# Two layers' filter products side by side, adaLN inside the first k and q units, and k's norm moved: a startup rearranged

## The chip, the core and the metric

The kernel runs on one core of one Trainium2 chip, as one program launched once. The metric is the device time of an execution in microseconds (us). Engines are named as in the profile: PE does the matmuls (PEld loads their weights), DVE and ACT the elementwise work, POOL and SP here almost only issue DMA transfers. All 16 DMA engines of the core serve the queues of SP and POOL.

## The reference

One step of a two-layer model on 256 latent and 128 context tokens of width 2048. Per layer: a shift, a scale and a gate come from a conditioning vector (adaLN), the normalised input is modulated by them and projected, and two branches share the result.

```python
shift, scale, gate = jnp.split(silu(c) @ w_ada + b_ada, 3)
h = rmsnorm(x, norm_g) * (1.0 + scale) + shift
q, k, v, g_att, hy_in, g_hy = jnp.split(h @ w_in, ...)
q = rmsnorm(q per head, q_g); k = rmsnorm(k per head, k_g)    # latent tokens: rotary as well
att = attend(q, k and cached k, v and cached v) * silu(g_att)
hy = hyena(hy_in, ...) * silu(g_hy)                           # long convolution through an FFT
x = x + gate * (concat(att, hy) @ w_out)
```

The long convolution needs a filter per layer. A small network over position features gives 64 hidden values per position; these are multiplied by a 64 x 2048 matrix (a forward and a backward filter of 1024 channels), weighted by a decay window, folded into one centred filter and Fourier transformed:

```python
hdn = sin(freq * (sin(freq * (z @ f_w1 + f_b1)) @ f_w2 + f_b2))     # L x 64
h = (hdn @ f_w3) * (exp(-t * deltas) + 0.05)                        # L x 2048
hf = rfft(fold(h[:, :1024], h[:, 1024:]))
```

The filters depend on weights only, so both layers' filters can be made at any time before they are used.

## The kernel before, in words

All matmul weights arrive in *units* of 1 MB, each as two halves of 512 KB that go into one of seven raw buffers (`RAWB`). SP issues the loads, in the order in which the program emits them; a load waits until its buffer has been released. There are adaLN units (function `ada_mm`; an "a" in `START`), units of k, q and v (kind "b", `b_mm`), and units of the other projections, which make up the main stream with v and the rest of q (kinds "a" and "o", `a_mm`). For the b units and the main stream the raw half is split into a rounded part `hi` (ACT, line 192) and a remainder `lo` (DVE, line 198), which releases the raw buffer; three matmuls (lines 765 to 767) then make up one exact product. An adaLN unit is multiplied as it is: four products, each on its own 32 columns of PE (line 249), and the raw halves are released by PE itself. Four adaLN units make a chunk of 512 outputs; the last copies the sums (line 255), and one step later `ada_fin` transposes them (line 262) and adds the bias. When shift and scale of a quarter of the features are there, `make_h` (lines 410, 414, 417) makes the modulated input for four of the 16 feature tiles.

Startup handles 40 units in the order that the string `START` writes out: 17 adaLN units, then k and q units with groups of 4, 4, 2, 2, 2 and 1 adaLN units between them, then the last k and the last q unit. k and q each have four units, and each accumulates into three banks of PSUM (128 tokens each). The last two units count no longer as startup.

Each unit is a *step* of a planner written in Python. In a step the program emits the loads for which buffers have come free (`load_main`), the unit's matmuls, and then background work from a list with a cost for each item, as long as a budget lasts: 2.0 for an adaLN unit (`BUD`), 0.8 for a b unit (`EB`), and an item is begun while any budget is left. A second list, `urgent`, holds work with the step at which it is due. `drain_bg` empties all lists at once.

The background list at startup is the making of the filters. For a layer `l`, a half of the channels `hf`, a position block `t` (two latent, one context) and the sum or difference `s` of forward and backward filter:

- `filt_h` (line 482): one product on 64 rows of PE, those of layer `l` (line 487), multiplied by the window on DVE (line 489) into one of six pieces of `pieces[hf]`; for two of the six, a row with the bias is added (line 491, loaded by POOL, line 466).
- `filt_H` (line 496): the transform of the latent part: two products (line 499), a copy on ACT (line 502), two combinations on DVE (503, 504) back into the pieces.
- `filt_Hc` (line 509): the same of the context part, one product (511) and one ACT copy (512).
- `spill` (line 516) writes finished pieces to memory, 256 KB each, from where line 694 fetches them later. Layer 0's pieces go through POOL's queue as soon as they are done. Layer 1's stay in their buffers and go through SP's queue, all twelve in a row, after `drain_bg` at the last k unit.

The list runs layer 0 half 0, layer 0 half 1, layer 1 half 0, layer 1 half 1; products of one group are emitted between the transforms of the group before it. `pieces[1]` lies in P3 and P4; P4 also receives k when it leaves PSUM.

When k's fourth unit is done, `b_evac` copies the three token blocks out of PSUM (line 779) and puts three calls of `qk_norm` into `urgent`, for this step, the next and the one after. `qk_norm` squares (536), sums (538), takes the root, scales (546), multiplies by the gain (547) and applies the rotary (556 to 561, the latent blocks only); one step later `tr4` transposes the block on PE (528). q does the same one step behind. The main stream after it (from 217.3 us on, 1296 us) is not edited by the change.

Of the kernel before, what the change touches and what calls it, by code (L numbers as in the profile page):

```python
# [13 lines left out]
ALU = mybir.AluOpType  # L14
# [23 lines left out]
AB = 1  # L38
AB0 = 1
FIN = 0  # L40
MB = 0
EB = 0.8
W0, W1, W2, W3, W4 = 6, 8, 4, 24, 0
R_Q = [0, 0, 0, 0, 2, 2, 4, 5]
# [26 lines left out]
def step_kernel(ctx, tc, xT, vec, cst, delta, zfeat, fw, ada, wb, wc, wo, ck, cv, qk1, yT, nk, nv):  # L71
# [171 lines left out]
    def ada_mm(u):  # L243
        l, ch, kc = u.kw["l"], u.kw["ch"], u.kw["kc"]
        if kc == 0:
            ada_bank[0] = adap.tile([128, 512], F32, name="adab", tag="bk")
        part = ada_bank[0]
        for t in range(4):
            mm(part[32 * t:32 * t + 32, :], scT[:, kc * 4 + t, :], u.raw[t // 2][:, (t % 2) * 512:(t % 2 + 1) * 512],  # L249
               start=(kc == 0), stop=(kc == 3))  # L250
        for h in range(2):
            release(u, h)
        if kc == 3:
            sb = tt()
            nc.scalar.copy(sb, part)
            (fins if FIN else urgent).append((state["step"] + 1, lambda: ada_fin(l, ch, sb)))
# [206 lines left out]
                              in_=fw[33 + 64 * l:33 + 64 * l + 64, 0:64])  # L463

    def load_hrow(l, hf):
        nc.gpsimd.dma_start(out=hrow[hf], in_=fw[289:290, (2 * l + hf) * 512:(2 * l + hf + 1) * 512])

    def filt_prep():
        for hf in range(2):
            load_hrow(0, hf)  # L470
# [7 lines left out]
    hsd = {}  # L478
    pieces = [[P1[:, 0:512], P1[:, 512:1024], P1[:, 2560:3072], P2[:, 3072:3584], P2[:, 3584:4096], P3[:, 2048:2560]],
              [P3[:, 2560:3072]] + [P4[:, 512 * i:512 * (i + 1)] for i in range(5)]]  # L480

    def filt_h(l, hf, t, s):

        b = bg_bank()
        w = w3s if s == 0 else w3d
        pr = slice(64 * l, 64 * l + 64)
        mm(b, hd2[pr, t * 128:(t + 1) * 128], w[pr, hf * 512:(hf + 1) * 512], start=True, stop=True)  # L487
        dst = pieces[hf][t * 2 + s]
        nc.vector.tensor_tensor(dst, b, win[:, t, hf * 512:(hf + 1) * 512], ALU.mult)
        if s == 0 and t != 1:  # L490
            nc.vector.tensor_tensor(dst[0:1, :], dst[0:1, :], hrow[hf], ALU.add)
            if t == 2 and l == 0:
                load_hrow(1, hf)
        hsd[hf, t, s] = dst

    def filt_H(l, hf, s):
        bs = [bg_bank() for _ in range(2)]
        for e in range(2):
            mm(bs[e], FL[:, s, e, :], hsd[hf, e, s], start=True, stop=True)  # L499
        t = tt()  # L500
        o, o2 = hsd[hf, 0, s], hsd[hf, 1, s]
        nc.scalar.mul(t, bs[0], 1.0 / LAT)
        nc.vector.scalar_tensor_tensor(out=o, in0=bs[1], scalar=1.0 / LAT, in1=t, op0=ALU.mult, op1=ALU.add)
        nc.vector.scalar_tensor_tensor(out=o2, in0=bs[1], scalar=-1.0 / LAT if s == 0 else 1.0 / LAT, in1=t,
                                       op0=ALU.mult, op1=ALU.add if s == 0 else ALU.subtract)
        if l == 0:
            spill(l, hf, s, (0, 1))

    def filt_Hc(l, hf, s):
        b = bg_bank()  # L510
        mm(b, FC[:, s, :], hsd[hf, 2, s], start=True, stop=True)
        nc.scalar.mul(hsd[hf, 2, s], b, 1.0 / CTX)
        if l == 0:
            spill(l, hf, s, (2,))

    def spill(l, hf, s, ts):
        for t in ts:
            (nc.gpsimd if l == 0 else nc.sync).dma_start(out=Hd[l][hf][:, 2 * t + s, :], in_=pieces[hf][t * 2 + s])


    qT = P1.rearrange("p (h t) -> p h t", h=8)
# [230 lines left out]
    def b_mm(u):  # L752
# [3 lines left out]
        for h in range(2):  # L756
            wh = u.hi[h].rearrange("p (k n) -> p k n", k=2)
            wl = u.lo[h].rearrange("p (k n) -> p k n", k=2)
            for m in range(3):
                for k in range(2):  # L760
                    kt = kc * 4 + h * 2 + k
                    ms = slice(m * 128, (m + 1) * 128)
                    first = kt == 0
                    last = kt == 15
                    mm(accs[g][m], hh[:, kt, ms], wh[:, k, :], start=first, stop=False)  # L765
                    mm(accs[g][m], hh[:, kt, ms], wl[:, k, :], start=False, stop=False)  # L766
                    mm(accs[g][m], hl[:, kt, ms], wh[:, k, :], start=False, stop=last)  # L767
                if u.mid and (h, m) != (1, 2):
                    run_bg(MB)

    def b_evac(u):
        l, g, kc = u.kw["l"], u.kw["g"], u.kw["kc"]
# [2 lines left out]
        for m in range(3):  # L775
            if g == 3:
                v_evac(l, m, accs[g][m])
            else:
                nc.scalar.copy((P4 if g == 2 else P3)[:, m * 512:(m + 1) * 512], accs[g][m])
# [140 lines left out]
    with tc.manual_schedule():  # L920
# [8 lines left out]
        at(11, rstd1)  # L929
        at(12, have_rstd)  # L930
        hs_t, H_t = [], []
        for l in range(NL):
            for hf in range(2):
                hs_t.append([(0.86, lambda l=l, hf=hf, t=t, s=s: filt_h(l, hf, t, s))
                             for s in (1, 0) for t in range(3)])
                H_t.append([(1.7, lambda l=l, hf=hf, s=s: filt_H(l, hf, s)) for s in (1, 0)] +
                           [(0.86, lambda l=l, hf=hf, s=s: filt_Hc(l, hf, s)) for s in (1, 0)])
        order = list(hs_t[0])
        for n in range(4):
            nh = hs_t[n + 1] if n < 3 else [None] * 6  # L940
            for k in range(4):
                order += [H_t[n][k]] + nh[(0, 1, 3, 5)[k]:(1, 3, 5, 6)[k]]
        for e in order:
            if e is not None:
                add(e[1], e[0], 2)
        last = None
        for i, u in enumerate(units + mains):
            load_main()
            startup = i < n_start
            u.mid = startup  # L950
            if startup or u.kind != "ada":
                state["step"] += 1
            if u.kind == "ada":
# [16 lines left out]
            if u.kind == "b" and u.kw["g"] == 2:  # L970
                kc = u.kw["kc"]
                if l == 1 and kc == 0:
# [1 line left out]
                    make_h(l, [0])  # L974
                    make_h(l, [1])
                    make_h(l, [2, 3])
                if kc == 3 and l == 0:
                    drain_bg()
                    for hf in range(2):
# [151 lines left out]
```

## Time and profile before

| what | value |
|---|---|
| time, median of 3 runs | 1515.55 us (1514.62 to 1516.08) |
| the profiled execution's own time | 1515.29 us |
| its span in the profile | 1513.5 us |
| PE busy | 1476.8 us, 98% of the span |
| DVE busy | 980.7 us, 65% |
| ACT busy | 578.0 us, 38% |
| granted clock of PE, mean | 0.989 |
| first k matmul, first matmul behind the last q unit | 87.9 us, 191.7 us |

A line of groups reads: line, engine, operation, what it writes <- what it reads, shapes, count | busy time, mean ns of one | idle time of the engine before them and who ended it. A matrix product of 32-bit numbers shows as two records (two passes). A line of the timeline reads: start, length, engine, line, operation, and in brackets the idle time before it and its cause. A line of the chain of waits gives start, length and what the path to the end was doing. A line of the waits gives who waited, for whom, total time, how often, the longest. A row of the windows gives the stretch, its length, busy time (and count) of PE, PEld, DVE, ACT and POOL, the granted clock, the DMA engines' busy share and the rate in GB/s.

### The profile page before, as it was taken

The numbers are of one execution on the slowest core, as the hardware profiler recorded it, in microseconds if no ns is written. First come the engines' busy times: TensorE is split into PE (matmuls) and PEld (weight loads), VectorE is DVE, ScalarE is ACT, GpSimd is POOL, SyncE is SP. The second block draws the span as 40 slices with busy tenths as digits, with TensorE's granted clock in tenths as the row PEclk, the third lists the DMA queues.
The fourth block names the chain that finished last, engine by engine and source line by source line (L and its number), as shares of the span: only waits on it lengthen the run. The fifth ranks groups of instructions, "written<-read, shape, count | busy, mean of one in ns | idle before, by whom it ended". The sixth has DMA issues, their size and how long they took to land.

```text
span 1513.5 us, 20685 instructions
## 1 busy us (share of the span) xinstructions
PE 1476.8 (98%) x8020; PEld 1298.3 (86%) x8020; DVE 980.7 (65%) x1618; ACT 578.0 (38%) x959; POOL 39.8 (3%) x77
## 2 busy tenths in 40 slices
PE   9998889999999999999999999999999999999996
PEld 5345667999998888999998888899999999999995
DVE  5743465677787656678777755776677847655444
ACT  2432454455432222235333554455543232234231
POOL 1100000000000000000111000000000000000000
PEclk9999999999999999999999999999999999999998
DMA  9977846444456576566776333544445343444422
GB/s 353 359 268 275 295 160 227 172 159 160 154 196 226 204 248 222 178 206 207 244 243 224 108 122 125 188 140 142 145 162 200 131 169 138 171 171 140 158 98 84
DMA packets 79211, 286.48 MB, mean 189 GB/s; under 512 B 9638, under 2 KB 9960, under 8 KB 78600
## 3 DMA queue, kind: packets, MB, share of 16 engines
q1 hardware_dynamic: 74264, 270.33, 51.1%
q0 software_dynamic: 4848, 14.82, 2.8%
q8 instruction: 63, 1.03, 0.3%
q14 instruction: 36, 0.29, 0.1%
HBM read 271.49 MB, written 13.63 MB: 188 GB/s over the span
## 4 chain that ended last, share of the span: by engine, by line
PE 92%; DMA 3%; DVE 3%; ACT 1%; issue 0%; SPq 0%; DVEq 0%; ACTq 0%
PE acc L790 21%; PE acc L792 21%; PE acc L791 21%; PE acc L765 5%; PE acc L766 5%; PE acc L767 5%; PE adab L249 3%; DMA raw<-in_wb 2%; DMA raw<-in_ada 2%; PE bgb L627 1%; PE bgb L610 1%; PE bgb L487 1%; PE bgb L718 1%; PE bgb L499 1%; DVE lo L198 1%; PE bgb L620 1%
## 5 line engine op out<-in xcount | busy, mean ns | idle before, releaser
L790 PE MATMUL acc<-hh,hi 128*128 128x384 f32 x1792 | 613.5, 342 | 0.0
L792 PE MATMUL acc<-hh,lo 128*128 128x384 f32 x1792 | 602.8, 336 | 0.0
L791 PE MATMUL acc<-hl,hi 128*128 128x384 f32 x1792 | 602.6, 336 | 0.0
L198 DVE TENSOR_TENSOR lo<-raw,hi 128x1024 fp32r<-128x1024 f32 x288 | 350.5, 1220 | 155.1 <-issue 56.1
L192 ACT CAST hi<-raw 128x1024 fp32r<-128x1024 f32 x288 | 301.1, 1046 | 349.3 <-issue 196.6
L790 PEld LDWEIGHTS acc<-hh,hi 128*128 128x128 f32 x1792 | 337.3, 188 | 17.1 <-issue 11.2
L791 PEld LDWEIGHTS acc<-hl,hi 128*128 128x128 f32 x1792 | 337.4, 188 | 3.2 <-issue 1.0
L792 PEld LDWEIGHTS acc<-hh,lo 128*128 128x128 f32 x1792 | 337.3, 188 | 0.0
L324 DVE SCALAR_TENSOR_TENSOR pa<-raw,scT,pa 128x512 f32<-128x512 f32 x330 | 225.9, 744 | 0.0
L765 PE MATMUL acc<-hi,hh 128*128 128x512 f32 x384 | 157.3, 410 | 5.0 <-ACT hh L414 2.6
L766 PE MATMUL acc<-lo,hh 128*128 128x512 f32 x384 | 154.3, 402 | 1.5 <-DVE lo L198 1.5
L767 PE MATMUL acc<-hi,hl 128*128 128x512 f32 x384 | 153.9, 401 | 0.0
L765 PEld LDWEIGHTS acc<-hi,hh 128*128 128x128 f32 x384 | 73.5, 191 | 30.9 <-ACT hh L414 4.5
L766 PEld LDWEIGHTS acc<-lo,hh 128*128 128x128 f32 x384 | 73.7, 192 | 19.4 <-DVE lo L198 2.4
L767 PEld LDWEIGHTS acc<-hi,hl 128*128 128x128 f32 x384 | 73.5, 192 | 18.4 <-DVE hl L417 0.5
L371 ACT ACTIVATE tt<-XM 128x384 f32<-128x384 f32 x48 | 24.8, 524 | 136.4 <-DVE XM L838 132.1
L838 DVE SCALAR_TENSOR_TENSOR XM<-acc,mod,xo 128x256 f32<-128x256 f32 x64 | 23.8, 413 | 64.5 <-PE acc L792 64.5
L249 PE MATMUL adab<-raw,scT 128*32 128x512 f32 x416 | 60.0, 603 | 3.2 <-DMA raw<-in_ada 3.2
L684 DVE SCALAR_TENSOR_TENSOR z<-acc,V,z 128x255 f32<-128x255 f32 (+1 forms) x64 | 25.2, 414 | 36.9 <-ACT z L680 35.7
L684 DVE SCALAR_TENSOR_TENSOR XM<-acc,V,XM 128x255 f32<-128x255 f32 (+1 forms) x64 | 25.2, 414 | 30.3 <-ACT XM L680 29.2
L684 DVE SCALAR_TENSOR_TENSOR x1c<-acc,V,x1c 128x255 f32<-128x255 f32 (+1 forms) x64 | 25.2, 414 | 26.2 <-ACT x1c L680 25.0
L801 DVE TENSOR_TENSOR XM<-XM,tt 128x384 f32<-128x384 f32 x16 | 8.9, 558 | 48.9 <-ACT tt L800 48.9
(160 smaller groups left out, 1072.1 us busy)
## 6 DMA issues: line engine op xcount, KB each, us to landing
raw<-in_ada SPq DMA_DIRECT2D x192, 512.0 KB, 5.2
raw<-in_wc SPq DMA_DIRECT2D x160, 512.0 KB, 3.9
raw<-in_wb SPq DMA_DIRECT2D x64, 512.0 KB, 4.8
raw<-in_wo SPq DMA_DIRECT2D x64, 512.0 KB, 4.4
P<-Hd SPq DMA_DIRECT2D x4, 1536.0 KB, 9.7
XM<-in_xT SPq DMA_DIRECT2D x4, 768.0 KB, 9.2
Hd<-P POOLq DMA_DIRECT2D x12, 256.0 KB, 6.1
Hd<-P SPq DMA_DIRECT2D x12, 256.0 KB, 7.1
```

The costliest lines, as they stand in the source:

```text
L192: nc.scalar.copy(u.hi[h], u.raw[h])
L198: nc.vector.tensor_tensor(u.lo[h], u.raw[h], u.hi[h].bitcast(F32), ALU.subtract)
L249: mm(part[32 * t:32 * t + 32, :], scT[:, kc * 4 + t, :], u.raw[t // 2][:, (t % 2) * 512:(t % 2 + 1) * 512], start=(kc == 0), stop=(kc == 3))
L324: nc.vector.scalar_tensor_tensor(out=acc, in0=w, scalar=sc, in1=acc, op0=ALU.mult, op1=ALU.add)
L371: nc.scalar.activation(sq[:, :T], XM[:, kt, :], AF.Square)
L684: nc.vector.scalar_tensor_tensor(out=out[:, o:o + n], in0=bank[:, i:i + n], scalar=w(k), in1=out[:, o:o + n], op0=ALU.mult, op1=ALU.add)
L765: mm(accs[g][m], hh[:, kt, ms], wh[:, k, :], start=first, stop=False)
L766: mm(accs[g][m], hh[:, kt, ms], wl[:, k, :], start=False, stop=False)
L767: mm(accs[g][m], hl[:, kt, ms], wh[:, k, :], start=False, stop=last)
L790: mm(b[:, :T], wh, hh[:, kt, :], start=(kt == 0), stop=False)
L791: mm(b[:, :T], wh, hl[:, kt, :], start=False, stop=False)
L792: mm(b[:, :T], wl, hh[:, kt, :], start=False, stop=(kt == 15))
```

## The change

Three things, all in startup.

1. The filter products of both layers are made together. One `filt_h` item (cost 1.02 instead of 0.86) now issues the product of layer 0 on rows 0 to 63 and that of layer 1 on rows 64 to 127 one after the other into two banks, and then both multiplies. `pieces` are kept by layer instead of by half: both layers' half 0 is made and transformed first, then half 1 into the same pieces. Half 0's pieces are spilled as soon as they are done, layer 0's on POOL, layer 1's on SP. Half 1's pieces are all spilled at the second k unit (`kc == 1`) instead of the fourth; there is a `drain_bg` at both.
2. While a startup k or q unit is multiplied, up to three of the adaLN units that follow it are issued inside it: after the first and the third token block of the first half, and after the second block of the second half. Such a unit has no step of its own any more.
3. k's three norms in layer 0 are due at the step itself, three steps later and four steps later, instead of zero, one and two.

```diff
@@ Unit
-            self.mid, self.of = False, None
+            self.mid, self.of, self.inter, self.done = False, None, [], False
@@ ada_mm
+        u.done = True
@@ filt_h
-    def filt_h(l, hf, t, s):
-
-        b = bg_bank()
+    def filt_h(hf, t, s):
+
+        bs = [bg_bank() for _ in range(NL)]
         w = w3s if s == 0 else w3d
-        pr = slice(64 * l, 64 * l + 64)
-        mm(b, hd2[pr, t * 128:(t + 1) * 128], w[pr, hf * 512:(hf + 1) * 512], start=True, stop=True)
-        dst = pieces[hf][t * 2 + s]
-        nc.vector.tensor_tensor(dst, b, win[:, t, hf * 512:(hf + 1) * 512], ALU.mult)
-        if s == 0 and t != 1:
-            nc.vector.tensor_tensor(dst[0:1, :], dst[0:1, :], hrow[hf], ALU.add)
-            if t == 2 and l == 0:
-                load_hrow(1, hf)
-        hsd[hf, t, s] = dst
+        c = slice(hf * 512, (hf + 1) * 512)
+        for l in range(NL):
+            pr = slice(64 * l, 64 * l + 64)
+            mm(bs[l], hd2[pr, t * 128:(t + 1) * 128], w[pr, c], start=True, stop=True)
+        for l in range(NL):
+            dst = pieces[l][t * 2 + s]
+            nc.vector.tensor_tensor(dst, bs[l], win[:, t, c], ALU.mult)
+            if s == 0 and t != 1:
+                nc.vector.tensor_tensor(dst[0:1, :], dst[0:1, :], hrow[l], ALU.add)
+                if t == 2 and hf == 0:
+                    load_hrow(l, 1)
@@ filt_H, filt_Hc
-        if l == 0:
+        if hf == 0:
             spill(l, hf, s, (0, 1))
...
     def spill(l, hf, s, ts):
         for t in ts:
-            (nc.gpsimd if l == 0 else nc.sync).dma_start(out=Hd[l][hf][:, 2 * t + s, :], in_=pieces[hf][t * 2 + s])
+            (nc.gpsimd if l == 0 else nc.sync).dma_start(out=Hd[l][hf][:, 2 * t + s, :], in_=pieces[l][t * 2 + s])
@@ b_mm
                 if u.mid and (h, m) != (1, 2):
-                    run_bg(MB)
+                    run_bg(0)
+                if u.inter and (h, m) in ((0, 0), (0, 2), (1, 1)):
+                    ada_mm(u.inter.pop(0))
@@ b_evac
-                urgent.append((state["step"] + m, lambda m=m: qk_norm(l, g, m)))
+                wait = (0, 3, 4)[m] if l == 0 and g == 2 else m
+                urgent.append((state["step"] + wait, lambda m=m: qk_norm(l, g, m)))
@@ the list, and the loop over the units
+        for hf in range(2):
+            hs_t.append([(1.02, lambda hf=hf, t=t, s=s: filt_h(hf, t, s)) for s in (1, 0) for t in range(3)])
+            H_t.append([x for s in (1, 0) for l in range(NL) for x in (
+                (1.7, lambda l=l, hf=hf, s=s: filt_H(l, hf, s)), (0.86, lambda l=l, hf=hf, s=s: filt_Hc(l, hf, s)))])
+        order = hs_t[0] + H_t[0][:5] + hs_t[1][:1] + H_t[0][5:7] + hs_t[1][1:2] + H_t[0][7:] + hs_t[1][2:] + H_t[1]
...
         for i, u in enumerate(units + mains):
+            if u.done:
+                continue
             load_main()
...
+            if startup and u.kind != "ada":
+                for v in units[i + 1:]:
+                    if v.kind != "ada":
+                        break
+                    u.inter.append(v)
...
-                if kc == 3 and l == 0:
+                if kc in (1, 3) and l == 0:
                     drain_bg()
-                    for hf in range(2):
+                if kc == 1 and l == 0:
+                    for j in range(NL):
                         for s in range(2):
-                            spill(1, hf, s, (0, 1, 2))
+                            spill(j, 1, s, (0, 1, 2))
```

More of the change, by code (lines that the diff above doesn't have):

```diff
@@ L40 @@
 FIN = 0
-MB = 0
 EB = 0.8
@@ L465, in load_hrow @@
     def load_hrow(l, hf):
-        nc.gpsimd.dma_start(out=hrow[hf], in_=fw[289:290, (2 * l + hf) * 512:(2 * l + hf + 1) * 512])
+        nc.gpsimd.dma_start(out=hrow[l], in_=fw[289:290, (2 * l + hf) * 512:(2 * l + hf + 1) * 512])
     def filt_prep():
-        for hf in range(2):
-            load_hrow(0, hf)
+        for l in range(NL):
+            load_hrow(l, 0)
         for t in range(3):
@@ L476, in filt_prep @@
             nc.vector.tensor_scalar(win[:, t, :], win[:, t, :], 0.05, None, ALU.add)
-    hsd = {}
     pieces = [[P1[:, 0:512], P1[:, 512:1024], P1[:, 2560:3072], P2[:, 3072:3584], P2[:, 3584:4096], P3[:, 2048:2560]],
               [P3[:, 2560:3072]] + [P4[:, 512 * i:512 * (i + 1)] for i in range(5)]]
-    def filt_h(l, hf, t, s):
-        b = bg_bank()
+    def filt_h(hf, t, s):
+        bs = [bg_bank() for _ in range(NL)]
         w = w3s if s == 0 else w3d
-        pr = slice(64 * l, 64 * l + 64)
-        mm(b, hd2[pr, t * 128:(t + 1) * 128], w[pr, hf * 512:(hf + 1) * 512], start=True, stop=True)
-        dst = pieces[hf][t * 2 + s]
-        nc.vector.tensor_tensor(dst, b, win[:, t, hf * 512:(hf + 1) * 512], ALU.mult)
-        if s == 0 and t != 1:
-            nc.vector.tensor_tensor(dst[0:1, :], dst[0:1, :], hrow[hf], ALU.add)
-            if t == 2 and l == 0:
-                load_hrow(1, hf)
-        hsd[hf, t, s] = dst
+        c = slice(hf * 512, (hf + 1) * 512)
+        for l in range(NL):
+            pr = slice(64 * l, 64 * l + 64)
+            mm(bs[l], hd2[pr, t * 128:(t + 1) * 128], w[pr, c], start=True, stop=True)
+        for l in range(NL):
+            dst = pieces[l][t * 2 + s]
[4 more added lines that the diff above has]
+                    load_hrow(l, 1)
     def filt_H(l, hf, s):
         bs = [bg_bank() for _ in range(2)]
-        for e in range(2):
-            mm(bs[e], FL[:, s, e, :], hsd[hf, e, s], start=True, stop=True)
+        o, o2 = pieces[l][s], pieces[l][2 + s]
+        for e, x in enumerate((o, o2)):
+            mm(bs[e], FL[:, s, e, :], x, start=True, stop=True)
         t = tt()
-        o, o2 = hsd[hf, 0, s], hsd[hf, 1, s]
         nc.scalar.mul(t, bs[0], 1.0 / LAT)
@@ L510, in filt_Hc @@
         b = bg_bank()
-        mm(b, FC[:, s, :], hsd[hf, 2, s], start=True, stop=True)
-        nc.scalar.mul(hsd[hf, 2, s], b, 1.0 / CTX)
-        if l == 0:
+        x = pieces[l][4 + s]
+        mm(b, FC[:, s, :], x, start=True, stop=True)
+        nc.scalar.mul(x, b, 1.0 / CTX)
+        if hf == 0:
             spill(l, hf, s, (2,))
@@ L517, in spill @@
         for t in ts:
-            (nc.gpsimd if l == 0 else nc.sync).dma_start(out=Hd[l][hf][:, 2 * t + s, :], in_=pieces[hf][t * 2 + s])
+            nc.gpsimd.dma_start(out=Hd[l][hf][:, 2 * t + s, :], in_=pieces[l][t * 2 + s])
     qT = P1.rearrange("p (h t) -> p h t", h=8)
@@ L931, in step_kernel @@
         hs_t, H_t = [], []
[L932 to L946, printed above, removed]
+        for hf in range(2):
[3 more added lines that the diff above has]
+        order = hs_t[0] + H_t[0][:5] + hs_t[1][:1] + H_t[0][5:7] + hs_t[1][1:2] + H_t[0][7:] + hs_t[1][2:] + H_t[1]
+        for cost, fn in order:
+            add(fn, cost, 2)
         for i, u in enumerate(units + mains):
+            if u.done:
+                continue
             load_main()
@@ L976, in step_kernel @@
                     make_h(l, [2, 3])
-                if kc == 3 and l == 0:
+                if kc in (1, 3) and l == 0:
                     drain_bg()
-                    for hf in range(2):
+                if kc == 1 and l == 0:
+                    for j in range(NL):
                         for s in range(2):
-                            spill(1, hf, s, (0, 1, 2))
+                            spill(j, 1, s, (0, 1, 2))
             if u.kind == "o" and u.kw["f"] == 0:
```

## The prediction

> **What bounds the kernel now.** I read the page first (PE busy 98% of the span), then cut the span into stages with the table of windows, because every edit lies in the first 220 us.
>
> ```profile
> span 1513.5 us, 20685 instructions
> core 0: us, PE busy (x) PEld busy (x) DVE busy (x) ACT busy (x) POOL busy (x), PEclk, DMA share, GB/s
> 18.90:49.00 30.10, 29.70 (x107) 8.55 (x106) 20.84 (x37) 11.82 (x20) 4.67 (x9) 1.00 1.03 414
> 49.00:87.90 38.90, 38.81 (x149) 13.00 (x149) 29.68 (x60) 16.78 (x31) 3.26 (x6) 1.00 0.83 305
> 87.90:168.70 80.80, 70.87 (x354) 45.26 (x352) 29.65 (x61) 22.59 (x36) 0.00 (x0) 1.00 0.77 276
> 168.70:187.40 18.70, 18.64 (x72) 14.48 (x72) 9.00 (x20) 8.62 (x16) 0.00 (x0) 0.91 0.94 332
> 187.40:192.40 5.00, 0.95 (x6) 0.74 (x5) 3.60 (x6) 4.98 (x10) 0.00 (x0) 0.78 0.13 54
> 192.40:205.30 12.90, 11.71 (x46) 9.18 (x44) 9.46 (x19) 6.66 (x16) 0.00 (x0) 0.82 0.23 81
> 217.30:1513.50 1296.20, 1277.38 (x7142) 1185.60 (x7138) 860.62 (x1388) 496.03 (x812) 30.43 (x56) 0.99 0.50 173
> ```
>
> To see here: up to 49 us PE and DMA are both full (share 1.03, 414 GB/s). From 49.0 to 87.9, when the first k unit starts, PE is full and DMA is not (0.83): PE is the bound. From 87.9 to 168.7 (k and q with adaLN units between) PE loses 9.9 us. Then come the last k and q units, a gap of 4 us, and two stretches in which the granted clock fell (0.91, 0.82). After 217.3 PE is busy 98.5% of the time; the change issues nothing there, so what startup saves should arrive whole at the end.
>
> **Filter products in pairs.** The chain of waits gives net costs on PE:
>
> ```profile
> 23.26 0.99 PE adab L249 x8
> 24.25 2.77 PE bgb L487 x6
> 28.02 1.91 PE bgb L499 x4
> 36.36 12.69 DMA raw<-in_ada
> 49.09 1.05 PE adab L249 x4
> 52.45 1.05 PE bgb L487 x2
> 55.55 1.05 PE bgb L511 x2
> ```
>
> A product on 64 rows (L487, two passes) costs 1.05 alone and 2.77 in threes, so about 0.86 each and 0.19 at the end of a group. Nothing before the change runs two products on two row halves. The bounds of a pair are 1.05 (full overlap) and 1.91 (none: what two products in a row cost, as in the L499 row). The nearest row is the adaLN unit: four products on four groups of columns, eight passes of about 0.6, in 0.99. That is four products for one, so I take 1.05 a pair, 1.91 for two pairs in a row.
>
> In strict order the two passes of each product would let only the middle passes of a pair overlap, three passes of 0.43 instead of two; against that speaks the L249 row, as eight ordered passes on four groups would take five times 0.43, not 0.99. The Trainium skill ("TensorE: Matmul & The Clock Gate", part 3, what overlaps and what doesn't) states such an order: matmuls start and end strictly in program order. By that rule the sum below would be 2.1 us smaller.
>
> How much reaches the path? Up to 49 us nothing does. The chain waits there for a transfer issued at 36.36 that lands at 49.05 behind a full queue, and the ninth adaLN unit (a8) waits for it. Counting the planner's budget of 2.0 by hand, the old list has done 13 single products, three H and two Hc by then; the new one (two pairs at 1.02 in a step) has done seven pairs, four H and three Hc in the same steps. What is left behind a8 is 11 products, 5 H, 6 Hc before, and 5 pairs, 4 H, 5 Hc after.
>
> ```profile
> L487 PE MATMUL bgb<-P,P 64*128 64x512 f32 x22 | 12.3, 641 | 0.0
> L499 PE MATMUL bgb<-P,C 128*128 128x512 f32 x20 | 9.3, 598 | 0.0
> L511 PE MATMUL bgb<-P,C 128*128 128x512 f32 x12 | 6.4, 627 | 0.0
> L489 DVE TENSOR_TENSOR P<-bgb,P 128x512 f32<-128x512 f32 x12 | 8.2, 685 | 2.7 <-PE bgb L487 2.7
> ```
>
> (Groups from 49 to 87.9, two records per product: 11, 10 and 6 products.) PE: 11 x 1.05 = 11.6 becomes 1.91 + 3 x 1.05 = 5.1, less one H (1.9) and one Hc (1.05): 38.9 - 6.5 - 2.95 = 29.4, so PE could reach k at 78.4. Three things push it back. Five more spills of 256 KB (0.63 us each at 414 GB/s) now come before a8 in a full DMA: up to 3 us. DVE, which still makes one multiply of 0.685 per product, had 29.7 us to do in this stage and hardly has less: from about 50 us that is 80, and it cannot run without gaps. And there is a new wait: the second half of the columns now reuses the same pieces two steps after their spill instead of a whole round later, and layer 1's spills moved from POOL's queue to SP's, behind the weights.
>
> ```profile
> L518 POOL DMA_DIRECT2D Hd<-P x12: 539/539/563, 31.0 to 63.1; - x12
> DMA to landing us min/median/max: 3.8/6.1/7.2
> L144 SPq DMA_DIRECT2D raw<-in_ada x41: 327/328/1169, 3.6 to 88.8; - x41
> DMA to landing us min/median/max: 3.7/8.3/13.9
> ```
>
> On POOL a spill landed after 6.1 us; in SP's queue transfers took 8.3, up to 13.9. So DVE stands at the first multiply of the second half from about 40 to 48 us, and sums of squares and the H combinations queue behind it. SP in turn waits for DVE before each spill, and the next weights wait behind SP. Seven half units of 512 KB in flight (1.27 us each, 9 us) cover most of that, and PE waits for a8 then anyway. I put the first k matmul at 82: **6 us saved** (0 if DMA or DVE sets it, 9 if PE does).
>
> **adaLN units inside k and q.** PE's losses between 87.9 and 168.7:
>
> ```profile
> PE adab L249 <- DMA raw<-in_ada: 2.4, 2, 1.2
> PE acc L765 <- ACT hi L192: 2.3, 2, 1.6
> PE bgb L262 <- ACT tt L255: 2.3, 2, 1.5
> PE acc L766 <- DVE lo L198: 1.5, 2, 0.8
> PE acc L765 <- ACT hh L414: 1.4, 1, 1.4
> ```
>
> Sum 9.9. The first four (8.5) have one cause: during the 8.4 us of k or q no adaLN buffer comes free, so the next unit lands late. Inside the unit three buffers' worth come free early; the last adaLN unit moves into q, so its copy (L255) is done when k needs it. The fifth (1.4, make_h before the last k) stays. Added: PE takes instructions in order, so where an inserted unit's data is late, the rest of k stands behind it. In the first k that is a18, whose second half is issued at a15's release and needs 3.7 us at least to land: I count 0.7. And 13 units now stand between matmuls of another shape:
>
> ```profile
> 131.35 1.85 PE adab L249 x16
> 205.35 1.07 PE L249 MATMUL adab<-raw,scT 128*32 128x512 f32 x8
> 206.34 0.50 PE L765 MATMUL acc<-hi,hh 128*128 128x512 f32 x1
> 206.68 0.39 PE L766 MATMUL acc<-lo,hh 128*128 128x512 f32 x1
> 206.91 0.40 PE L767 MATMUL acc<-hi,hl 128*128 128x512 f32 x1
> ```
>
> One alone takes 0.99, and the next matmul 0.34 to the following start instead of 0.23, with some 0.09 ahead: 1.18. The second of two adds 0.86. The groups 4, 4, 2, 2, 2, 1 become singles: 2 x 0.96 + 3 x 0.32 = 2.9 more. The skill's "TensorEngine Tiling" (key properties) says that changing the tiling mode drains the engine; the rows agree, at 0.3 us a time. Spills of the second half at the second k: layer 0's on POOL go earlier, when their data is ready; layer 1's six (3.9 us) stand on SP before the next weights, where DMA has room (0.77). 9.9 - 1.4 - 0.7 - 2.9 = **4.9 saved** (1 to 7).
>
> **Last k and q, and k's norm.** In 168.7:187.4 two units take 18.7 us at clock 0.91, where 36 matmuls at 0.233 make 8.4 each: 1.9 lost after the stalls of 1.5 and 1.4 us. With only 1.4 left I count 1.8 saved (0 to 1.9). Then:
>
> ```profile
> 182.98 1.56 ACT L779 COPY P<-acc 128x512 f32<-128x512 f32 x3 [6.81 <-DMA Hd<-P]
> L518 SPq DMA_DIRECT2D Hd<-P x12: 320/584/2415, 168.2 to 179.1; - x12
> 191.69 1.08 PE L528 MATMUL bgb<-C,P 128*128 128x128 f32 x4 [4.05 <-DVE P L561]
> 204.79 0.63 PE L528 MATMUL bgb<-C,P 128*128 128x128 f32 x4 [1.19 <-ACT tt L536]
> ```
>
> k's copies waited 6.8 us for twelve spills on SP to leave the buffer. These now go 50 us earlier. From the first copy to k's transpose is 8.7 us; the third copy, 1.0 later (three in 1.56 at 0.6 each), can start when k ends, so the chain takes 7.7 after k, and q gives 8.4 of cover: the 4.05 goes. So does the 1.19, as only q's block is normed in that step; k's second block now shares the step of q's third, where the smaller 0.3 may stay. Without the gap the clock should hold: 192.4:205.3 ran 8.4 us of matmuls in 10.5. 4.05 + 1.19 + 2.1 = **7.3 saved** (4 to 8).
>
> **Sum.** 6 + 4.9 + 1.8 + 7.3 = 20.0. The profiled execution took 1515.29 us (1.8 outside its span), 0.26 under the median of 1515.55: 1515.3 - 20.0 = 1495.3. All low ends together give 1510, all high ends 1489.
>
> **Rivals.**
> - *The pairs do not overlap* (the change does not do what it says). For: no row shows row halves together. Against: the column groups. Five pairs at 0.86 more: 1499.6. Chance 0.07.
> - *The passes keep strict order*, three per pair: five times 0.43 more, 1497.4. For and against as above. 0.05.
> - *DMA and DVE set the whole first stage*: all 6 are lost, 1501.3. For: share 1.03 to 49 us, DVE 29.7 in a stage of 33. Against: 0.83 afterwards. 0.15.
> - *The norm chain does not fit under q.* Its slack is 0.7 us; if splits of the next weights come between, half of the tail and its clock loss stay: 1499. 0.10.
> - *The ring of SP and DVE starves PE.* At the new spills SP waits for DVE, DVE for an earlier spill's landing, the weights for SP. If none of the three rounds (steps 6, 8, 9) is covered and each costs a landing of 8.3, startup is 25 us longer: 1520. It turns slower from 20 us, so from two and a half rounds on. For: the queue is full just then. Against: nine us of weights in flight, and a8 is late anyway. 0.06.
> - *Forecast*, 0.57, with a little beyond it where PE alone sets the first stage.
>
> **Numbers.** Likeliest 1495.3. A measurement tells about 0.2% (3 us) from no change. The range takes in the first four rivals and the bound of the first stage: 1489.5 to 1503. Faster 0.92, same 0.02, slower 0.06.
>
> **What would show it.** L487's successors on two row halves starting within 0.1 us, a pair near 1.05; the first k matmul near 82 us; between there and the last k about 73 us, PE waiting under 3 in all; no wait of the k copies for Hd, PE less than 1 us idle after q, clock 1.0 from 160 to 217; the stage behind unchanged at 1296. A first k later than 88 us, a DMA share well below 1.0 before 49 us, or DVE waiting for Hd for more than 10 us would make me wrong.

## The result and the profile after

The changed kernel took 1500.45 us (median of four, 1498.11 to 1505.12) against 1515.09 us (1513.79 to 1516.08): a ratio of 0.9903, 95% interval 0.9883 to 0.9923. It is 14.6 us faster, inside the range; 20.0 were forecast. The profiled execution took 1501.41 us. Of all the executions behind the numbers below, one was slow and is left out: 3757 us, of the kernel with pairs on the same rows.

One thing has to be put right first. The section on the change, and the prediction with it, misread one line of the diff: they put layer 1's spills on SP, and the line is printed so there. The line that ran is `nc.gpsimd.dma_start(out=Hd[l][hf][:, 2 * t + s, :], in_=pieces[l][t * 2 + s])`, so **all 24 spills go through POOL's queue**. One run below is the kernel that the prediction reckoned with. Its time is the same, but the place of half 1's spills turns out to matter more than most of what was argued about.

The windows of the changed kernel, cut at these landmarks: the filters' start, the second half of a8 (the ninth adaLN unit), the first k matmul, the last k unit, the third unit of the main stream. One row more, 50.0 to 53.3 us, lies inside the second stretch. The columns are those of the prediction's table:

```profile
span 1499.6 us, 20692 instructions
18.80:50.10 31.30, 27.34 (x115) 8.28 (x114) 23.38 (x41) 12.57 (x22) 6.32 (x13) 1.00 1.03 414
50.00:53.30 3.30, 3.11 (x10) 1.12 (x12) 1.94 (x4) 1.05 (x3) 1.08 (x2) 0.50 1.03 420
50.10:82.10 32.00, 31.48 (x140) 11.02 (x140) 24.80 (x54) 15.03 (x30) 6.26 (x12) 0.95 0.87 319
82.10:164.70 82.60, 75.93 (x353) 44.57 (x353) 31.24 (x62) 22.56 (x35) 1.75 (x4) 0.96 0.92 334
164.70:202.30 37.60, 37.56 (x172) 28.44 (x172) 26.11 (x47) 22.80 (x44) 0.00 (x0) 1.00 0.46 161
202.30:1499.60 1297.30, 1278.10 (x7150) 1186.29 (x7146) 865.22 (x1399) 500.75 (x826) 31.06 (x57) 0.99 0.50 173
```

The kernel before, from its last k unit to the third unit of the main stream:

```profile
168.70:217.30 48.60, 42.97 (x180) 32.31 (x180) 30.68 (x59) 27.24 (x57) 0.54 (x1) 0.89 0.59 204
```

To see: the second half of a8 runs about 1 us later than before (50.2 against 49.1), but from there to the first k matmul it is 32.0 us instead of 38.8, although the granted clock was at one half for some 3 us of it. The stretch from the first k matmul to the last k unit is *longer* than before (82.6 against 80.8), at a mean clock of 0.96 instead of 1.00. Behind the last k unit PE is full (37.56 of 37.60) at clock 1.00, where before it was busy for 42.97 of 48.60 at 0.89. By the starts of the first matmul of each unit (us):

| stretch | before | after | saved | forecast |
|---|---|---|---|---|
| start to first k unit | 87.89 | 82.11 | 5.8 | 6 |
| first k to last k unit | 80.82 | 82.59 | -1.8 | 4.9 |
| last k unit to third unit of the main stream | 48.62 | 37.61 | 11.0 | 9.1 (1.8 + 7.3) |
| third unit to the end | 1296.20 | 1297.33 | -1.1 | 0 |

They sum to 13.9, the difference of the spans. The last row moves by as much among the kernels below, which all have the same main stream (1295.5 to 1297.8), so what it shows is scatter.

The chain of waits of the changed kernel (start, length, what the path did) holds the good step and the bad one:

```profile
20.40 1.92 PE bgb L488 x8
...
55.38 1.06 PE bgb L488 x4
...
80.17 10.22 DMA raw<-in_ada
...
90.44 1.92 PE adab L249 x4
```

L488 is the new line of the filter products: one pair (four passes) takes 1.06 us, two in a row 1.92. The transfer issued at 80.17 is the second half of a18. (That is the prediction's name for the eighteenth adaLN unit, the first one inside the first k unit; a8, by another count, is the ninth.) It lands 10.2 us later, and the rest of k stands behind it. PE's waits between 20 and 220 us, summed (total, times, longest):

```profile
PE adab L249 <- DMA raw<-in_ada: 7.8, 5, 3.3
PE acc L768 <- DVE lo L197: 1.5, 2, 0.8
PE acc L767 <- ACT hh L414: 1.4, 1, 1.4
```

Of the 7.8, 3.3 and 0.4 are a18's; the other 4.1 lie between 41 and 51 us, at the eighth and ninth adaLN units, the last two of them (1.55 and 1.34 us) just ahead of the fall of the clock at 50 us. What stood against a18's transfer is seen in the tile view of the spills (count, duration, first and last start),

```profile
L520 POOL DMA_DIRECT2D Hd<-P x24: 539/542/566, 34.5 to 84.8; - x24
```

and in the DMA view of 82 to 90 us (queue, kind: packets, MB, share of the 16 engines; q1 is SP's queue, q0 POOL's):

```profile
DMA packets 953, 3.33 MB, mean 416 GB/s; under 512 B 144, under 2 KB 144, under 8 KB 952
...
q1 hardware_dynamic: 475, 1.75, 53.4%
q0 software_dynamic: 477, 1.57, 48.3%
```

The program places half 1's spills at the second k unit (118 us), but POOL waits for little except their data (2.5 us in all for earlier spills to land), and issues all twelve between 75 and 85 us, just when a18 is wanted. POOL's queue then gets about half of a full rate (1.57 of 3.33 MB). PE stood idle for 3.29 us, and the granted clock fell towards the end of it, as the windows of that place show:

```profile
86.00:88.00 2.00, 0.00 (x0) 0.00 (x0) 1.76 (x5) 0.43 (x2) 0.00 (x0) 0.87 1.02 412
90.00:92.00 2.00, 1.57 (x6) 0.19 (x4) 0.58 (x2) 0.09 (x1) 0.00 (x0) 0.50 1.03 418
```

The Trainium skill ("TensorE: Matmul & The Clock Gate", Part 1) states that PE falls to half rate after an idle window of about 3.4 us. The length fits: the clock stayed at 0.5 from 87.5 to 94.3 us, twice 3.4. The condition does not: here the clock fell after 2.7 us of idle time, and at 50 us behind two waits of 1.55 and 1.34 us with matmuls between them, so less idle time was enough.

In the tail, k's copies out of PSUM (L783) no longer wait for spills, and start right behind the matmuls that they copy. The same view of the timeline, 160 to 190 us, ACT:

```profile
171.02 0.57 ACT L783 COPY P<-acc 128x512 f32<-128x512 f32 x1
172.31 0.59 ACT L783 COPY P<-acc 128x512 f32<-128x512 f32 x1 [0.72 <-PE acc L769]
```

### The profile page after: what moved, and what is told of

Read it like the earlier page. It is cut to its first block, busy times and chain, and to the rows that moved or that the text cites. A ratio compares the mean times of both kernels' runs of the same rounds, so it can differ in the third digit from the quotient of the medians.

```text
span 1499.6 us, 20692 instructions
## 1 busy us (share of the span) xinstructions
PE 1467.3 (98%) x8020; PEld 1292.0 (86%) x8020; DVE 980.0 (65%) x1618; ACT 577.3 (38%) x959; POOL 46.3 (3%) x89
## 3 DMA queue, kind: packets, MB, share of 16 engines
q8 instruction: 63, 1.03, 0.3%
## 4 chain that ended last, share of the span: by engine, by line
PE 94%; DMA 4%; DVE 1%; ACT 1%; issue 0%; SPq 0%; DVEq 0%; ACTq 0%
PE acc L795 21%; PE acc L797 21%; PE acc L796 21%; PE acc L767 6%; PE acc L768 6%; PE acc L769 6%; PE adab L249 3%; DMA raw<-in_ada 2%; PE bgb L629 1%; PE bgb L612 1%; PE bgb L720 1%; PE bgb L622 1%; DMA XM<-in_xT 1%; DMA raw<-in_wb 1%; PE bgb L530 1%; DVE XM L854 1%
## 5 line engine op out<-in xcount | busy, mean ns | idle before, releaser
L795 PEld LDWEIGHTS acc<-hh,hi 128*128 128x128 f32 x1792 | 336.9, 188 | 17.1 <-issue 11.2
L249 PE MATMUL adab<-raw,scT 128*32 128x512 f32 x416 | 65.4, 617 | 8.1 <-DMA raw<-in_ada 8.1
L249 PEld LDWEIGHTS adab<-raw,scT 128*32 128x32 f32 x416 | 9.8, 108 | 38.0 <-issue 18.4
```

Source lines behind the costliest of these rows:

```text
L795: mm(b[:, :T], wh, hh[:, kt, :], start=(kt == 0), stop=False)
```

## The experiments

My theory after the result: the change does what it says, and its insertion of adaLN units is worth what was forecast, but the lump of half 1's spills on POOL's queue takes it back (a late a18, then a half clock). The main rival: the insertion itself costs more than it saves, since it puts PE's order at the mercy of every late adaLN half. A second question was which of the two edits cleared the tail. Three chips were used, one for each group of runs; ratios are against the kernel before on the same chip.

**Half 1's spills through SP.**

```
-            nc.gpsimd.dma_start(out=Hd[l][hf][:, 2 * t + s, :], in_=pieces[l][t * 2 + s])
+            (nc.gpsimd if hf == 0 else nc.sync).dma_start(out=Hd[l][hf][:, 2 * t + s, :], in_=pieces[l][t * 2 + s])
```

> The changed kernel, but half 1's twelve spills go through SP's queue at the second k unit (in line behind the weights) instead of POOL's, where they run as soon as their data is ready, 75 to 96 us. Theory 1, the spills take half of the DMA rate just when a18 is wanted inside the first k: first k matmul stays near 82, a18's second half lands by 85, PE waits under 1 us there, the clock does not fall at 87 to 94 us, the stage from first k to last k shrinks from 82.6 to about 76 us, and the time is about 6 us under the changed kernel's 1500.5: 1494 to 1496. Rival, a18 is asked for too early whatever the spills do, because its buffer comes free only when a15 is done: the wait of 3 us and the fall of the clock stay, 1500 to 1501.

Measured: 1502.9 us, ratio 0.9914 (0.9900 to 0.9927). The time missed. Two rows for each kernel show why; first the changed kernel's first k unit and second q unit (each up to the start of the next k or q unit):

```profile
82.10:104.20 22.10, 17.61 (x73) 8.42 (x73) 6.74 (x13) 5.23 (x8) 1.75 (x4) 0.85 1.01 402
130.10:141.30 11.20, 11.20 (x58) 7.25 (x56) 2.69 (x3) 2.48 (x3) 0.00 (x0) 1.00 0.79 266
```

then the same two units of this kernel:

```profile
80.30:96.30 16.00, 14.87 (x73) 7.62 (x73) 6.23 (x13) 4.75 (x8) 0.00 (x0) 1.00 0.98 349
123.70:143.90 20.20, 14.52 (x57) 8.50 (x56) 3.20 (x4) 2.74 (x4) 0.00 (x0) 0.83 0.87 297
```

The first k unit lost its stall: 16.0 us at clock 1.00 instead of 22.1 at 0.85. The second half of a18 landed after 5.94 us instead of 10.22, and PE waited 0.36 us for it. So the spills on POOL were the cause of the stall. But twelve spills in a row on SP, at the second k unit, hold up the adaLN halves that are issued behind them, and a stall of the same kind appears 44 us later, in the timeline of PE:

```profile
131.96 1.92 PE L249 MATMUL adab<-raw,scT 128*32 128x512 f32 x4 [5.68 <-DMA raw<-in_ada]
```

What follows: 3 MB in one lump cost some 6 us on POOL (22.1 against 16.0) and 9 on SP (20.2 against 11.2).

**Layer 1's spills through SP** (the kernel that the prediction reckoned with): the same line with `l == 0` for `hf == 0`.

> The changed kernel with layer 1's spills of both halves on SP, layer 0's on POOL (the queues that the prediction reckoned with). Theory 1: six spills instead of twelve run beside the first k, so a18's wait falls from 3.3 to 1 or 2 us; DVE's wait for a spill to leave the buffers of half 1 grows from 3.9 to about 8 us, with the first k matmul at 82 to 84: 1496 to 1500. Rival, SP and DVE wait for one another in a ring: first k later than 88 us, time over 1505.

Measured: 1501.03 us, 0.9903 (0.9889 to 0.9916), the changed kernel's own ratio. a18 waited 3.2 us, as there, and not the 1 to 2 us expected, so with six spills on POOL it waited about as long as with twelve. a8, behind layer 1's spills in SP's queue, waited 3.7 (timeline of PE):

```profile
50.72 1.12 PE L249 MATMUL adab<-raw,scT 128*32 128x512 f32 x4 [3.69 <-DMA raw<-in_ada]
```

The misreading thus did not move the time as a whole, and the ring of SP and DVE that was feared there cost a stall of 3.7 us, not three landings of 8.3; the first k matmul came at 82.74.

**No insertion**: the list of units to be inserted stays empty, and adaLN units follow k and q as before.

```
-            if startup and u.kind != "ada":
+            if False:
```

> The changed kernel with the adaLN units after the k and q units, as before. Theory 1: without a18 inside the first k the spills cost nothing there; PE loses again some 8 us between the units, but no clock: the stage from first k to last k takes 80 to 81 us as it did before the change, against 82.6 with insertion, and the time is 1498 to 1500. Had the insertion brought its 4.9 us, this would be 1505. Rival, insertion itself is what costs (changes of tiling, PE in order): 1494 to 1496.

Measured: 1504.8 us, 0.9927 (0.9913 to 0.9940), slower than both theories said. The windows' rows of its first k unit, with the adaLN units behind it, and of the stretch from first to last k unit:

```profile
80.50:101.30 20.80, 16.75 (x72) 8.07 (x72) 8.28 (x20) 5.89 (x11) 1.92 (x4) 1.00 1.03 417
80.50:169.50 89.00, 75.08 (x352) 46.26 (x352) 31.15 (x62) 22.72 (x35) 1.92 (x4) 0.98 0.80 298
```

and PE's waits from 30 to 190 us:

```profile
PE adab L249 <- DMA raw<-in_ada: 7.6, 9, 1.6
PE bgb L262 <- ACT tt L255: 3.7, 3, 1.8
PE acc L768 <- DVE lo L197: 2.9, 4, 0.8
PE acc L767 <- ACT hi L191: 2.5, 3, 1.5
```

89.0 us, not 82.6: the insertion saves 6.4 us in its stretch, so the rival that it costs on balance falls. In time it is worth about 4 us (span 1503.7 against 1499.6), near the 4.9 of the forecast. What is missing was lost beside it, and with or without insertion: here the first k unit and its adaLN units took 20.8 us with the DMA engines full (1.03), where before they took 16.1 (87.89 to 103.98 us). That the spills would cost nothing there without insertion, as the first theory had it, was wrong.

**k's norms in their old steps** (`wait = m` for all), and the two tail edits each alone in the kernel before: **the spread norms alone** (its line for `wait`), and **the early spills alone** (layer 1's twelve, on SP as before, at the second k unit instead of the fourth).

> The changed kernel with k's three norms due at 0, 1 and 2 steps as before. If the gap of 4.05 us behind the last q unit went because the spills had left k's buffer early, and only the 1.19 one step later because of the norms: 1 to 2 us slower than the changed kernel, 1501.5 to 1503, no gap before the first transpose of k. If the spread norms did it: 5 to 8 us slower, 1506 to 1508, with the gap back.

> The kernel before with nothing changed but k's three norms, due at 0, 3 and 4 steps. Theory: the gap of 4 us behind the last q unit stays, because k's copies still wait for the spills until 183 us; the 1.2 us gap a step later goes: 1513 to 1514.5, 1 to 2 us less than before. If the spread norms are what the tail gain comes from, 4 to 6 us less: 1509 to 1511.

> The kernel before, with nothing changed but that layer 1's twelve spills are sent on SP at the second k unit instead of the last. Theory (from the run with the old norms, whose gap came back one step later): the gap behind the last q unit goes, since k's copies no longer wait 6.8 us for the spills, but one of nearly the same size stands one step later, where a block of k and one of q are normed together, so only about 3 us come of it; and the twelve transfers hold up the weights behind the second k unit, as in the run with half 1 on SP, which costs up to 6: 1513 to 1519. Were the early spills the cause of the whole tail gain, as the prediction had it (6 of 7.3 us): 1509 to 1510.

Measured: without the spread 1505.5 us, 0.9933 (0.9921 to 0.9945); the spread alone 1512.01, 0.9964 (0.9951 to 0.9977); the early spills alone 1516.64, 0.9994 (0.9981 to 1.0007), which is no change. The first two lie between the two outcomes that were written down for each. The rows that follow are PE's timeline where it transposes the normed blocks, with the idle time ahead of a row in brackets. Without the spread:

```profile
193.18 0.63 PE L530 MATMUL bgb<-C,P 128*128 128x128 f32 x4 [3.94 <-DVE P L563]
```

The spread alone:

```profile
191.04 1.08 PE L528 MATMUL bgb<-C,P 128*128 128x128 f32 x4 [4.29 <-DVE P L561]
201.95 0.60 PE L528 MATMUL bgb<-C,P 128*128 128x128 f32 x4
```

The early spills alone:

```profile
189.90 0.60 PE L528 MATMUL bgb<-C,P 128*128 128x128 f32 x4
203.26 1.09 PE L528 MATMUL bgb<-C,P 128*128 128x128 f32 x4 [3.92 <-DVE P L561]
```

With the spread alone the first gap stays (k's copies still wait for the spills) and the later ones go. With the early spills alone, in either kernel, the first gap goes and one of the same size opens one unit later, in the steps where by the code a block of k and one of q are normed together. From the start of the last q unit to the third main unit the four cases took 38.3 us (neither), 35.3 (spread alone), 36.4 (spills alone), 28.8 (both): each alone gives 2 or 3 us, both give 9.5. (These are single profiles; by the ratio of times, the spread alone gives 3.5 to 7 us.) The kernel with early spills alone also paid for its lump: SP issued nothing else for 10.8 us, the weights behind it came late, and PE stood for 3.4 us ahead of the third k unit. SP's timeline:

```profile
123.97 10.79 SPq L518 DMA_DIRECT2D Hd<-P x12
```

**Pairs on the same rows.** Layer 1's product is taken on rows 0 to 63 as well, so that nothing can overlap; layer 1's filter is then made from layer 0's hidden values.

```
-            pr = slice(64 * l, 64 * l + 64)
+            pr = slice(0, 64)
```

> The changed kernel with both products of a pair on rows 0 to 63 (layer 1's filter is then made of layer 0's hidden values, so that part of the computation is changed). They can't overlap: two products cost 1.91 instead of 1.06. If PE sets the first stage after a8: five pairs by 0.86, the first k 4 us later, 86, and the time 1504 to 1505. If DMA and DVE set it: first k within 1 us of 82, time as the changed kernel's 1500.5. Up to 49 us no difference in either.

The chain of waits of that kernel:

```profile
43.63 1.91 PE bgb L488 x4
...
56.77 3.63 PE bgb L488 x8
```

A pair costs 1.91, not 1.06: the overlap of the row halves is real, and it is complete. What it is worth is less sharp. The first k matmul came at 84.2 us, against 80.1 to 82.1 in the nine profiles of kernels that share the changed first stage. The two latest of the nine, 81.9 and 82.1, are those in which the clock fell at 50 us; the other seven lie at 80.1 to 80.6, and against these it is 3.6 to 4.1 us, where the five pairs behind a8 at 0.85 make 4.3. The time, 1504.05 us, ratio 0.9906 (0.9883 to 0.9928), does not show it: the changed kernel's own ratio was 0.9903, and on this chip, where the changed kernel itself was not run, the kernel before scattered from 1514 to 1522.

**Half 1's spills spread out.** On SP, three each at the second and third k and q units.

```
+        late = [(j, s) for j in (1, 0) for s in range(2)]
...
+                if u.kw["kc"] > 0:
+                    j, s = late.pop(0)
+                    spill(j, 1, s, (0, 1, 2))
```

> The changed kernel with half 1's twelve spills on SP, three each at the second and third k and q units. Theory 1 (spills cost where they stand in one lump beside weights that PE wants at once): no wait over 1.5 us from first k to last k but the 1.4 of make_h, clock 1.0 throughout, that stage 75 to 77 us, time 1493.5 to 1496. Rival: the DMA engines are simply full there (share 0.92), so a wait of 3 us or more turns up at another unit: 1499 to 1502.

Measured: 1496.88 us, 0.9869 (0.9847 to 0.9891), with 81.7 us in the stretch instead of the expected 75 to 77. The profile is of an execution of 1500.84 us, 4 us above the median, so the median's stretch may be shorter than 81.7. In the stretch no long stall and no half clock are left, yet in this execution it hardly became shorter. The timeline says what came in their place. In this kernel the first inserted unit of each k and q unit ran in two pieces:

```profile
127.85 1.05 PE L249 MATMUL adab<-raw,scT 128*32 128x512 f32 x4
129.19 1.05 PE L249 MATMUL adab<-raw,scT 128*32 128x512 f32 x4 [0.29 <-DMA raw<-in_ada]
133.17 1.06 PE L249 MATMUL adab<-raw,scT 128*32 128x512 f32 x8
```

Its second half came late. By the code, the program splits the first half of the *next* k or q unit ahead of the current one, so that unit's buffer stands ahead of the inserted units' buffers in the order in which free buffers are handed to new loads, although it comes free after theirs. The second half that ran at 129.19 was issued only at 124.24, 3.6 us before its unit's first half was multiplied.

**Own units first.** While units are inserted, the split of the next k or q unit comes behind them. This was run with the spread spills, with the changed kernel's lump, and with the spread spills on POOL's queue; the changed kernel itself ran beside them.

```
-            if near:
+            if near and not u.inter:
                 split(u.nxt, 0)
...
             if near:
+                split(u.nxt, 0)
                 split(u.nxt, 1)
```

> The spills of half 1 spread as in the run before (three each on SP's queue at the second and third k and q units), and the first half of the next k or q unit is split behind the inserted adaLN units instead of ahead of them, so that its buffer no longer stands ahead of theirs. Theory 1 (an inserted unit costs 2.0 to 3.0 us instead of 1.08 only because its second half is loaded late, since the next k or q unit's split hands the buffers out of turn): the first inserted unit of each k and q unit falls to about 1.1 us, six units by 1.0 to 1.9, so the stretch from the first k unit to the last goes from 81.7 to 74-77 us and the time to 1491-1495. Rival (those units wait for the transfers as such, since the adaLN units' bytes don't come faster): the extras fall, but waits for adaLN weights or for k and q weights of the same length come in their place; the stretch stays at 80-82 us and the time at 1496-1500.

> The changed kernel with nothing but the order of the splits turned as in the run above; the spills of half 1 stay in one lump on POOL. Theory 1 (the lump is what makes the first inserted unit of the first k unit wait, since it takes half of the transfers' rate while that unit's second half is under way): the wait of some 3 us there and the half clock behind it stay, the other first units lose 0.3 to 1.0 us each, and the time is 1498-1500.5. Rival (the order in which buffers are handed out was the cause of that wait, too): the wait goes, the stretch from the first k unit to the last falls from 82.6 to about 76 us, and the time is 1493-1495.

> The changed kernel once more, beside the others on one chip: 1498-1502, ratio 0.988 to 0.992. It gives the others a neighbour on the same chip, and no theory expects anything else.

> As the first run of this call, but the twelve spills go through POOL's queue, three each at the same units. Theory 1 (what counts is when the spills' bytes come, not by which queue): the same as the first run within 1 us. Rival (POOL's queue takes half of the rate from SP's wherever it has bytes to move, while on SP's queue the spills wait their turn behind weights that were asked for earlier): waits for weights of 0.5 to 1.5 us behind each of the four lots, 2 to 5 us longer than the first run.

Measured:

| kernel | us | ratio (95%) | first k to last k |
|---|---|---|---|
| changed kernel again | 1500.23 | 0.9895 (0.9877 to 0.9913) | 83.2 |
| own units first, lump on POOL | 1499.09 | 0.9883 (0.9865 to 0.9902) | 80.3 |
| own units first, "spread" on POOL | 1498.02 | 0.9877 (0.9859 to 0.9895) | 81.6 |
| own units first, spread on SP | 1493.59 | 0.9846 (0.9828 to 0.9864) | 77.1 |

The last one beats the kernel before by 22.5 us and the changed kernel by 6.6. Its waits of PE from 30 to 190 us:

```profile
PE adab L249 <- DMA raw<-in_ada: 3.3, 6, 1.3
PE acc L767 <- ACT hh L414: 1.4, 1, 1.4
```

The unit that ran in two pieces before now runs in one, at 125.34, like the unit behind it, which is shown with its neighbours in PE's timeline:

```profile
129.01 0.39 PE L769 MATMUL acc<-hi,hl 128*128 128x512 f32 x1
129.34 1.07 PE L249 MATMUL adab<-raw,scT 128*32 128x512 f32 x8
130.33 0.50 PE L767 MATMUL acc<-hi,hh 128*128 128x512 f32 x1
```

and its windows' row of the stretch:

```profile
80.40:157.50 77.10, 73.77 (x353) 43.67 (x353) 31.04 (x62) 22.76 (x35) 0.00 (x0) 1.00 0.99 369
```

Three of the six first units now run in one piece, and the next k matmul starts 1.32 us after the one ahead of the unit, instead of 0.23. The first three still wait. Of the two edits the order alone gave 1.1 us, which these intervals do not tell from nothing (a18's wait stayed, at 2.9 us, as the first theory had it), and the spreading on SP's queue 5.5 on top of it. What the order adds to the spreading is not shown for certain either: 0.9869 became 0.9846, on another chip, and the intervals overlap. The DMA share of the stretch is 0.99 now, so what is left there is probably the transfers as such, as the rival held.

The run on POOL's queue did not ask what it was meant to ask. Its spills stand at four units of the program, but POOL does not wait for PE, and issued them all by 88.7 us (tile view of the spills):

```profile
L520 POOL DMA_DIRECT2D Hd<-P x24: 542/542/566, 33.5 to 88.7; - x24
```

a18 waited 3.4 us, as with the lump. So whether spread spills on POOL would disturb less or more than on SP stays open; that a place in the program does not spread them there is shown.

## Why the prediction was right, and where it was not

**The filter products.** Right in the cost of a pair and in its cause. A pair took 1.06 us (forecast 1.05), two pairs 1.92 (1.91), and the first k matmul came at 82.11 (82). The rivals of no overlap (1.91 a pair) and of strict order of passes (1.48 a pair) both fall on these rows, and the pairs on the same rows show what no overlap looks like. The rule cited for the second, that matmuls end strictly in program order (the Trainium skill, "TensorE: Matmul & The Clock Gate", Part 3), gave 1.48 as the prediction used it; the measurement decides against that use. In the trace the first passes of a pair's two products start within 0.01 us of each other, and so do their second passes: the passes interleave, which the prediction did not consider, while the products as wholes may well keep their order. (The sum that the prediction calls 2.1 us smaller by that rule is the sum saved, which would be 17.9.)

That the first k matmul came within 0.1 us of the forecast is in part luck. Of the three things that were to push k back, the spills ahead of a8 did little (its second half ran 1.1 us later; up to 3 were forecast). The new wait of DVE was there: a multiply stood 3.90 us for a spill's landing, until 45.7 us. It cost PE nothing that shows, as PE waited for adaLN weights around then. What the prediction did not have is the fall of the clock at 50 us, 3.4 us long, some 1.6 us of work. In a second profile of the same kernel (the changed kernel again) the clock held there, and k began at 80.12, so that 7.8 us were saved and not 5.8.

**The insertion.** This is the step that failed: its term for a18 was far too small. The forecast was 9.9 - 1.4 - 0.7 - 2.9 = 4.9 us saved; the stretch became 1.8 longer. The mechanism was right: the kernel without insertion is 6.4 us longer there, and PE's waits fell from 9.9 to 6.7. The price of one inserted unit was about right as well (1.18 forecast; 1.32 - 0.23 = 1.09), and so was the term of 2.9 for all of them: in the last kernel above, whose clock holds in this stretch, PE is busy there for 73.77 us against 70.87 before. Wrong was the term of 0.7 for a18, "whose second half ... needs 3.7 us at least to land": it took 10.2. With POOL quiet beside it (half 1's spills through SP) the same half took 5.94 and cost a wait of 0.36, so the 0.7 would have held without the lump. In the changed kernel a18 cost 3.7 us of waits, and the first k unit ran the next 6.8 us at half clock, some 3 us more. Two sentences of the prediction led there. It said that spills on POOL go earlier, when their data is ready, but never asked what else is on its way then; and it found room for the others, those that it put on SP, in a DMA share of 0.77, which is a mean over 80 us. Where the spills came, the share was 1.01. Nor was that mean a fixed thing: in the best kernel above the stage ahead and this one are 7.5 and 3.7 us shorter than before, the same bytes have to come in less time, and the share is 0.99. Two of the prediction's signs did not show, both here: about 73 us in this stretch (its own sum, 80.8 - 4.9, gives 75.9; it became 82.6), and PE waiting for less than 3 us in it (6.7).

**Last k, last q and the norms.** Forecast 9.1 us; 11.0 measured. The mechanism holds as it was told: the copies no longer wait, the gap and the half clock behind it go. Between the two rows of this stretch that are shown with the result, PE's idle time falls by 5.6 us (4.05 + 1.19 forecast) and its busy time by 5.4 (1.8 + 2.1 forecast, all of it clock); the granted clock there goes from 0.89 to 1.00. Its two parts were not additive, though. The prediction gave 4.05 to the spills and 1.19 to the spread; alone they give 1.9 and 3.0, as the stretch from the last q unit to the third main unit shows, since either edit alone leaves a gap of 4 us in some step, with its clock loss.

**Rivals that did not come.** DMA and DVE did not set the whole first stage (5.8 of 6 saved). The chain of the norm does fit under q. The ring of SP and DVE could not form in the changed kernel, which has no spills on SP; in the kernel that has layer 1's there, it cost one stall of 3.7 us at a8, a place that is late before and after as well. The total was inside the range because the tail gave 1.9 us more than forecast and only one term was far off.

## What to carry to other kernels

A transfer that is issued by an engine with nothing else to wait for goes when its data is ready, wherever it stands in the program; ask what else is on its way at that moment, and take the DMA share of that moment, not of the stage. When work is put in line behind a load on an in-order engine, price the load by the landing times of a full queue, and add the clock that a stall of 3 us costs (here 3.4 or 6.8 us at one half). Two edits against one gap should be priced together: each alone may only move it.

## What was not expected of the hardware

- Two products of 32-bit numbers on 64 rows each, on the two row halves of PE, take 1.06 us together, no longer than one alone (1.05), two passes each.
- With both queues full, POOL's and SP's transfers shared 416 GB/s nearly evenly (1.57 and 1.75 MB in 8 us), and a weight half of 512 KB, issued at 80.17 us, took 10.2 us to land, against 5.9 with POOL's queue quiet.
- A stall of 3.3 us cost another 3 us by the clock: it stayed at one half for 6.8 us. The price is not fixed: behind a18's stall the half clock lasted 6.8 us in three profiles (stalls of 2.93, 3.29 and 3.31 us) and 3.4 us in three others (2.86, 3.17 and 3.43).
- The clock also fell without a long stall: at 50 us behind two waits of 1.55 and 1.34 us. In the second profile of the same kernel the two waits were 1.52 and 0.86 us, and it held.
